# Attention branch projection by seven products of quarters, with the sums of both factors made during the mLSTM

## The chip, the cores and the metric

The kernel runs on one core of one Trainium2 chip. The metric is the device time of one execution in microseconds. Before the change three runs took 1968.49, 1973.42 and 1973.98 us (median 1973.42).

## The reference, cut to what matters

One layer of a diffusion backbone on 1024 tokens of width 1024. Two token mixers work side by side on the same normed input, a windowed attention and a bidirectional mLSTM. Each one's output goes through a projection of its own, is gated, and the two are added:

```
ml = mlstm_readout(ht, mo, ml_norm_w)      # per head of 256: hn = ht * rsqrt(mean(ht^2) + eps) * w; hn * sigmoid(mo)
y  = sigmoid(ga) * (att @ w_branch_att) + sigmoid(gm) * (ml @ w_branch_ml)
x  = x + g1 * (y @ w_out)                  # then the ConvFFN on x, with its own residual
```

All matrices are 32-bit floats. `att`, `ml` and `y` are 1024 x 1024, and so are the three weights. The change concerns `att @ w_branch_att`, and the factor `rsqrt(mean(ht^2) + eps)` of the mLSTM's readout.

## The kernel before, in words

The stages follow one another in `layer_kernel`: startup and context, attention, mLSTM, tail (both branch projections, output projection, second norm), ConvFFN. Every matrix product is made with three matmuls: each operand is split in a high part (a copy on ScalarE, line 44) and a low part (a subtraction on VectorE, line 49), and high x high, high x low, low x high are added in PSUM (`mm3`, lines 90 to 92). The ConvFFN already makes its products by a scheme with seven products of quarters (`product`, lines 1397 to 1399).

A planner orders the instructions of each engine when the kernel is built: an instruction that is written earlier has priority, and one for which data and a buffer are there goes ahead of one that still waits. On the chip each engine then runs its own list in that fixed order. `tc.issue_after(x)` keeps the instructions of a block behind `x` on x's engine. A tile of a pool with `bufs=n` waits until the one n before it has been read for the last time. Loads and stores are issued from SyncE's queue (`nc.sync`) or from ScalarE's (`nc.scalar`).

**The mLSTM** goes head by head (four heads). `proj_kv` makes k and v for all tokens, `proj_q` and `trans_k` make q and the turned k, `states` the first chunk states, and `core` the rest of the chunks of both directions: score products S, outputs o and i, state updates dC. `proj_o` projects the output gate into `sg` (two tiles of 4 x 256 a partition; line 769 writes them), and its matmuls fill TensorE between the small ones of the core. `readout` (lines 1002 to 1015) then handles eight blocks of 128 tokens, one by one: a square with a sum on ScalarE (L1012), scale and power -0.5 on GpSimd (L1013, L1014), and the product with factor and gate on VectorE (L1015). The last of these is kept as `E.turned`. `turn` transposes the result on TensorE (L1023), scales it (L1025) and stores it as `mlT_d` (L1026), in DRAM.

**The attention branch projection** is the first part of `stage_tail`. The attention's output lies turned in DRAM (`attT_d`, 1024 features x 1024 tokens). `load_T` loads it in 16 pieces of 128 x 512 and splits them (`aTh`, `aTl`); `load_w` loads a half of the weight (512 columns) in pieces of 128 x 1024 elements and splits those (`wba0`, `wba1`). Then 16 tiles of 128 columns x 512 tokens follow, each a sum over 8 pieces of 128 features with three matmuls each, in one of two PSUM banks. Each tile's gate (`sga_d`, loaded on ScalarE's queue, L1143) goes through a sigmoid (L1176) and is multiplied with the tile (L1177), and the result is stored to `y1_d` (L1179). Behind these the planner is told to put the loads (L1161) and splits of the mLSTM's output (`mT`) for the next stage. From tile 11 on the first half of the next weight is loaded (`wbm0`).

**The mLSTM branch projection** has the same form (`ym`, gate `sgm`, lines 1199 to 1215): it adds the tile read back from `y1_d`, and VectorE also makes the sums of the modulation (`mod_product`, L210 to L215).

The lines that the prediction speaks of besides: L70 loads the mLSTM's projection weights from SyncE's queue, L1076 the tail's weights, L1116 the attention's output, L1196 the gate row `g1b`.

Of the kernel before, what the change touches and what calls it, by code (L numbers as in the profile page):

```python
# [42 lines left out]
def copy_act(nc, out, in_, scale=1.0):  # L43
    nc.scalar.activation(out, in_, AF.Copy, scale=scale)  # L44


def split_from(nc, hi, lo, src, eng="v"):
    copy_act(nc, hi, src)
    (nc.vector if eng == "v" else nc.gpsimd).tensor_tensor(lo, src, hi.bitcast(F32), op=ALU.subtract)  # L49

# [629 lines left out]
def stage_mlstm(E, st):  # L680
# [4 lines left out]
    psd = E.psx_s.enter_context(tc.tile_pool(name="ps_d", bufs=2, space=PSUM, reuse_waits="tile"))  # L685
    mp = st.enter_context(tc.tile_pool(name="ml1", bufs=1, reuse_waits="tile"))
# [315 lines left out]
    def readout(h):  # L1002
        hf, sgs = H[h]["hf"], H[h]["sg"]
        for t in halves(h):
            if h < MLH - 1:
                nc.scalar.activation(sgs[t], sgs[t], AF.Sigmoid)
            for c in range(4):
                cc = 4 * t + c
                x = hf[:, cc]
                rr = rp.tile([P, 2], F32, tag="rr", name=f"rr{h}_{cc}", bufs=8)  # L1010
                junk = rp.tile([P, 512], F32, tag="mo", name=f"rj{h}_{cc}", bufs=2)
                nc.scalar.activation(junk[:, :DV], x, AF.Square, accum_out=rr[:, 0:1])  # L1012
                nc.gpsimd.tensor_scalar(rr[:, 0:1], rr[:, 0:1], 1.0 / DV, EPS, op0=ALU.mult, op1=ALU.add)  # L1013
                nc.gpsimd.tensor_tensor(rr[:, 1:2], rr[:, 0:1], expo[:, 0:1], op=ALU.pow)  # L1014
                E.turned = nc.vector.scalar_tensor_tensor(x, x, rr[:, 1:2], sgs[t][:, c], op0=ALU.mult, op1=ALU.mult)  # L1015
# [11 lines left out]

    gate_math()
# [6 lines left out]
    proj_q(0)  # L1035
    decays(0)
    for h in range(MLH):
# [9 lines left out]
        if h + 1 < MLH:  # L1047
            proj_q(h + 1)
            trans_k(h + 1)


def stage_tail(E, st):
# [26 lines left out]
    def load_w(src, nm, gate=None, ks=range(2), raws=None):  # L1079
        out = []  # L1080
        for k4 in ks:
            raw = (raws or load_raw(src, nm, [k4]))[k4]
            for k2 in range(2):
# [4 lines left out]
                split_from(nc, h, lo, raw[:, 2 * k2 : 2 * k2 + 2].rearrange("p k c -> p (k c)"))  # L1088
# [16 lines left out]
    def load_T(src, nm, pools, ts=(0, 1), r=None, ks=range(KT)):  # L1105
        r = r or [[], []]
        for t in ts:
            for k in ks:
                if nm == "aT" and t == 0 and k >= 4:

                    if k % 2 == 0:
                        two = op4(f"{nm}r{k}_{t}", F32)
                    raw = two[:, k % 2 * 512 : k % 2 * 512 + 512]
                else:
                    raw = op2(f"{nm}r{k}_{t}", F32)
                E.last = nc.sync.dma_start(raw, src[k * P : (k + 1) * P, t * 512 : (t + 1) * 512])  # L1116
                hl = [x512(f"{nm}{x}{k}_{t}", pool=pools[t][k // 4]) for x in "hl"]
                split_from(nc, hl[0], hl[1], raw)
                r[t].append(hl)
        return r  # L1120

# [8 lines left out]
    def place(i):  # L1130
        n, t, c = tiles[i]
        r0 = n * 512 + c * P
        return slice(r0, r0 + P), slice(t * 512, (t + 1) * 512)

    def ahead(pool, src, tag, nm, bufs):
        got, todo = {}, list(range(16))

        def take(i):
            while todo and todo[0] <= i + 3:
                j = todo.pop(0)  # L1140
                got[j] = pool.tile([P, 512], F32, tag=tag, name=f"{nm}{j}", bufs=bufs)
                rs, ts = place(j)
                nc.scalar.dma_start(got[j], src[rs, ts])  # L1143
            return got.get(i)

        return take

    w = load_w(A["w_ba"][0], "wba0", ks=(0,))
    with tc.issue_after(E.turned.ins):
        aT = load_T(attT_d, "aT", ((0, 1), (2, 6)), (0,), ks=range(4))  # L1150
        w += load_w(A["w_ba"][0], "wba0", ks=(1,))
        load_T(attT_d, "aT", ((0, 1), (2, 6)), (0,), aT, range(4, 8))
    gate = ahead(gp, sga_d, "sg", "sga", 6)
    gate(0)
    load_T(attT_d, "aT", ((0, 1), (2, 6)), (1,), aT)
# [13 lines left out]
    for i, (n, t, c) in enumerate(tiles):  # L1169
        if i == 8:  # L1170
            with tc.issue_after(E.last.ins):
                w = load_w(A["w_ba"][1], "wba1")
        sg = gate(i)
        ps = mm_tile(f"ya{i}")
        mm3(nc, ps, w, aT[t], sl(c * P, P), sl(0, 512))
        ac = nc.scalar.activation(sg, sg, AF.Sigmoid)  # L1176
        dv = nc.vector.tensor_tensor(sg, ps, sg, op=ALU.mult)  # L1177
        rs, ts = place(i)
        sto = nc.sync.dma_start(y1_d[rs, ts], sg)  # L1179
        with tc.issue_after(ac.ins), tc.issue_after(dv.ins), tc.issue_after(sto.ins):  # L1180
            ml_split(i - 2 - 2)
            ml_load(i - 2)
        if i == 11:
            with tc.issue_after(sto.ins):
                wm = load_w(A["w_bm"][0], "wbm0")

# [6 lines left out]
    for i in range(16, 18 + 2):  # L1193
        ml_split(i - 2 - 2)
        ml_load(i - 2)
    nc.sync.dma_start(g1b, E.g_d[0].to_broadcast([P, D]))  # L1196
# [598 lines left out]
```

## Time and profile before

| What | Value |
|---|---|
| Runs | 1968.49, 1973.42, 1973.98 us |
| The profiled execution | 1969.57 us |
| Its span (first to last instruction) | 1967.6 us |
| Granted TensorE clock | 0.999 |
| Branch projection of the attention, first matmul to the next stage's first | 1054.93 to 1145.99 us |
| Waits of TensorE with a named releaser from 690 to 1240 us, the three largest | o for num 2.4, dC for C 1.9, dC for kwl 1.6 us |

The profile is one execution, taken by the hardware profiler. A row of the time line has the start, the duration, the engine (PE is TensorE, PEld its weight loads, DVE VectorE, ACT ScalarE, POOL GpSimd, SPq and ACTq the queues that issue transfers), the line of the kernel, the operation, `out<-in`, shapes and count; in square brackets stands how long the engine had been idle before it, and which instruction released it. Neighbouring rows of one engine overlap, since an instruction starts while the one before it drains: what one costs in a row of equal ones is the distance between starts. Rows of groups have the busy time in all, the mean in ns, and the idle time before. Rows of transfers end with the median time from issue to landing.

### The profile page before, as it was taken

To read this page: it belongs to the slowest core of one execution; us is meant where nothing else is said; L and a number is where in the kernel's file an instruction comes from. 1 tells how busy PE (TensorE), PEld (TensorE's weight loads), DVE (VectorE), ACT (ScalarE), POOL (GpSimd) and SP (SyncE) were. 2 spreads that over 40 slices of the span, in tenths; PEclk is the share of its full clock that TensorE was granted. 3 is DMA by queue.
4 is the path that set the end of the run, shared out by engine and by line. 5 is a ranking of instruction groups with operands and counts; after the bars stand their busy time and mean duration, and the time that the engine had idled before them with its cause. 6 is when DMAs were issued, how large, how long until landed. Compare 5 with 4: busy or idle time off the path is not lost.

```text
span 1967.6 us, 28480 instructions
## 1 busy us (share of the span) xinstructions
PE 1927.2 (98%) x10108; PEld 1649.0 (84%) x10108; DVE 1360.1 (69%) x2734; ACT 965.5 (49%) x1891; POOL 337.2 (17%) x578
## 2 busy tenths in 40 slices
PE   8999999999999999999999999999999999999999
PEld 3988888888888889998997888887888888888887
DVE  2767878868777574646465356559988988996564
ACT  4845556556556354444445332246544454465441
POOL 1223424333332232232221000010000000000000
PEclk9999999999999999999999999999999999999999
DMA  8731222222222211212108664732355444489651
GB/s 307 235 122 55 79 69 73 80 62 79 62 62 81 64 57 39 78 33 79 33 30 272 193 232 149 268 118 75 121 190 203 177 166 174 168 298 336 228 175 64
DMA packets 124013, 264.94 MB, mean 135 GB/s; under 512 B 13904, under 2 KB 38112, under 8 KB 121056
## 3 DMA queue, kind: packets, MB, share of 16 engines
q1 hardware_dynamic: 115232, 247.41, 36.9%
q10 hardware_dynamic: 8640, 15.73, 2.4%
q8 instruction: 79, 1.29, 0.3%
q14 instruction: 62, 0.51, 0.1%
HBM read 197.48 MB, written 65.61 MB: 134 GB/s over the span
## 4 chain that ended last, share of the span: by engine, by line
PE 80%; DVE 7%; DMA 7%; ACT 4%; issue 2%; POOL 1%; SPq 0%; ACTq 0%; POOLq 0%; DVEq 0%
PE pa L1397 4%; PE pa L1399 4%; PE pa L1398 4%; PE pt L623 3%; PE g L92 3%; PE g L91 2%; PE g L90 2%; DMA wmb<-in_w_modB 2%; PE dx L1397 2%; PE dx L1398 2%; PE dx L1399 2%; PE pb L1399 2%; PE pb L1398 2%; PE pb L1397 2%; PE po L617 2%; PE kv L90 2%
## 5 line engine op out<-in xcount | busy, mean ns | idle before, releaser
L604 POOL TENSOR_SCALAR P<-P,st 128x640 f32<-128x640 f32 (+1 forms) x128 | 115.2, 918 | 260.2 <-DVE st L602 177.7
L595 ACT ACTIVATE P<-P,st 128x640 f32<-128x640 f32 (+1 forms) x128 | 102.5, 801 | 24.7 <-DVE st L591 23.7
L591 DVE CUSTOM_DVE_ANT_0 P<-s,maskA,nsink 128x640 f32<-128x640 f32 (+1 forms) x112 | 103.1, 920 | 9.4 <-PE s L588 7.9
L49 DVE TENSOR_TENSOR pl<-pt,ph 128x512 fp32r<-128x512 f32 x152 | 100.8, 686 | 10.2 <-ACT ph L44 9.1
L44 ACT ACTIVATE ph<-pt 128x512 fp32r<-128x512 f32 x152 | 87.5, 597 | 37.1 <-PE pt L623 33.1
L90 PE MATMUL g<-hH,fh 128*128 128x512 f32 x256 | 102.7, 401 | 0.6 <-ACT fh L44 0.6
L92 PE MATMUL g<-hH,fl 128*128 128x512 f32 x256 | 100.6, 393 | 0.4 <-DVE fl L49 0.4
L91 PE MATMUL g<-hL,fh 128*128 128x512 f32 x256 | 100.5, 393 | 0.0
L623 PE MATMUL pt<-ident,P 128*128 128x128 f32 x608 | 92.3, 273 | 3.5 <-POOL P L604 3.1
L90 PE MATMUL pq<-w1h,hH 128*128 128x384 f32 (+1 forms) x256 | 87.1, 340 | 0.2 <-DVE t L543 0.2
L90 PE MATMUL kv<-w1h,hH 128*128 128x384 f32 x256 | 86.2, 338 | 1.1 <-ACT w1h L44 1.1
L92 PE MATMUL pq<-w1h,hL 128*128 128x384 f32 (+1 forms) x256 | 86.7, 339 | 0.0
L91 PE MATMUL kv<-w1l,hH 128*128 128x384 f32 x256 | 86.5, 338 | 0.0
L91 PE MATMUL pq<-w1l,hH 128*128 128x384 f32 (+1 forms) x256 | 86.5, 338 | 0.0
L92 PE MATMUL kv<-w1h,hL 128*128 128x384 f32 x256 | 86.2, 337 | 0.0
L623 PEld LDWEIGHTS pt<-ident,P 128*128 128x128 f32 x608 | 71.1, 140 | 11.5 <-POOL P L604 6.5
L90 PE MATMUL mo<-w1h,hH 128*128 128x256 f32 x256 | 72.7, 284 | 0.4 <-ACT sg L769 0.2
L92 PE MATMUL mo<-w1h,hL 128*128 128x256 f32 x256 | 72.2, 282 | 0.0
L91 PE MATMUL mo<-w1l,hH 128*128 128x256 f32 x256 | 72.1, 282 | 0.0
L49 DVE TENSOR_TENSOR dfl<-drf,dfh 128x512 fp32r<-128x512 f32 x55 | 38.0, 691 | 47.4 <-ACT dfh L44 47.4
L1535 ACT ACTIVATE cv<-ua,vecT 128x1024 f32<-128x1024 f32 x22 | 27.4, 1244 | 85.1 <-DVE ua L1508 85.1
L1397 PE MATMUL dx<-dwh,dfh 128*128 128x512 f32 x176 | 68.5, 389 | 0.0
(559 smaller groups left out, 6309.3 us busy)
## 6 DMA issues: line engine op xcount, KB each, us to landing
ur<-in_w_up SPq DMA_DIRECT2D x22, 1024.0 KB, 5.0
wmb<-in_w_modB SPq DMA_DIRECT2D x64, 256.0 KB, 2.9
f_d<-cv SPq DMA_DIRECT2D x22, 512.0 KB, 2.6
wm<-in_w_modA SPq DMA_DIRECT2D x16, 512.0 KB, 8.4
fr<-in_w_g SPq DMA_DIRECT2D x32, 256.0 KB, 3.1
drf<-fs_d SPq DMA_DIRECT2D x15, 512.0 KB, 5.6
drw<-wt_d SPq DMA_DIRECT2D x14, 512.0 KB, 6.3
w1b<-in_w_cx SPq DMA_DIRECT2D x16, 388.0 KB, 4.3
```

What stands on the lines that cost most here:

```text
L44: nc.scalar.activation(out, in_, AF.Copy, scale=scale)
L49: (nc.vector if eng == "v" else nc.gpsimd).tensor_tensor(lo, src, hi.bitcast(F32), op=ALU.subtract)
L90: nc.tensor.matmul(ps, lh[:, ls], rh[:, rs], start=start and i == 0, stop=False)
L91: nc.tensor.matmul(ps, lh[:, ls], rl[:, rs], start=False, stop=False)
L92: nc.tensor.matmul(ps, ll[:, ls], rh[:, rs], start=False, stop=stop and i == n - 1)
L591: nc.vector.tensor_tensor_reduce(pm[:, :W], ps[:, off : off + W], mask[:, :W], scale=ss[:, h : h + 1], scalar=nsink[:, hh : hh + 1], op0=A ...
L595: nc.scalar.activation(pm[:, :W], pm[:, :W], AF.Exp, bias=st4[:, h : h + 1], scale=-1.0, accum_out=st4[:, 4 + h : 5 + h])
L604: nc.gpsimd.tensor_scalar(Ps[h][:, :W], Ps[h][:, :W], st4[:, 12 + h : 13 + h], 1.0, op0=ALU.mult, op1=ALU.mult)
L623: nc.tensor.transpose(pt[:, h * P : (h + 1) * P], Ps[h][:, kb * P : (kb + 1) * P], ident)
L1397: nc.tensor.matmul(ps, lh, rh, start=start and i == 0, stop=False, skip_group_check=True)
L1398: nc.tensor.matmul(ps, lh, rl, start=False, stop=False, skip_group_check=True)
L1399: nc.tensor.matmul(ps, ll, rh, start=False, stop=stop and i == n - 1, skip_group_check=True)
```

## The change

1. *Seven products.* Both factors of `att @ w_branch_att` are cut in quarters of 512 x 512 (features by tokens, features by columns). Four sums of the quarters of each factor are formed, and seven products of 512 x 512 x 512 replace the eight: with b the turned attention output and w the weight, the pairs in `BR` below. A product needs 4 PSUM banks; banks are taken from four pools in two sets (`bankx`, `banky`), which products share in turns, so that two of the additions of the scheme are done in PSUM. The others are done by VectorE into eight tiles, `u2` and `u4`.
2. *Sums in the mLSTM.* `branch_sums` is called eight times: three times before the first head's `decays`, three after the first head, two after the second. A call loads four pieces of 128 x 512 (ScalarE's queue) into the two `sg` tiles of the output gate, makes four sums on VectorE and stores them (SyncE's queue) in `S_ba` or `T_at` in DRAM.
3. *Loads of the stage.* 14 steps, each with two transfers of 512 KB (factor and weight, two k each), each split in two parts per operand; two steps ahead of the matmuls. The operands' tiles, raw and split, come from the same pools as before.
4. *Order around it.* One half of the results stays in `u2` and `u4` for the next stage and isn't stored and read again. Ten of the loads of `mT` come with steps 4 to 13, the rest in the first tiles of the next stage, where `g1b` now follows the weight. That stage uses three PSUM banks in turns in place of two. Gates are prefetched into 8 tiles in place of 6.
5. *Norm factors.* The readout squares four blocks first, makes their four factors with two GpSimd instructions on 128 x 4, and then multiplies the four.

The diff, cut to its core:

```diff
@@ stage_mlstm, readout
+            rr = rp.tile([P, 8], F32, tag="rr", name=f"rr{h}_{t}", bufs=2)
             for c in range(4):
-                cc = 4 * t + c
-                x = hf[:, cc]
-                rr = rp.tile([P, 2], F32, tag="rr", name=f"rr{h}_{cc}", bufs=8)
...
-                nc.gpsimd.tensor_scalar(rr[:, 0:1], rr[:, 0:1], 1.0 / DV, EPS, op0=ALU.mult, op1=ALU.add)
-                nc.gpsimd.tensor_tensor(rr[:, 1:2], rr[:, 0:1], expo[:, 0:1], op=ALU.pow)
-                E.turned = nc.vector.scalar_tensor_tensor(x, x, rr[:, 1:2], sgs[t][:, c], op0=ALU.mult, op1=ALU.mult)
+                nc.scalar.activation(junk[:, :DV], hf[:, 4 * t + c], AF.Square, accum_out=rr[:, c : c + 1])
+            nc.gpsimd.tensor_scalar(rr[:, 0:4], rr[:, 0:4], 1.0 / DV, EPS, op0=ALU.mult, op1=ALU.add)
+            nc.gpsimd.tensor_tensor(rr[:, 4:8], rr[:, 0:4], expo[:, 0:4], op=ALU.pow)
+            for c in range(4):
+                x = hf[:, 4 * t + c]
+                E.turned = nc.vector.scalar_tensor_tensor(x, x, rr[:, 4 + c : 5 + c], sgs[t][:, c], op0=ALU.mult, op1=ALU.mult)
@@ stage_mlstm, new
+    def branch_sums():
+        which, i = SUMS.pop(0)
+        two = [rp.tile([P, 4, DV], F32, tag="sg", name=f"bs{which}_{i}_{j}", bufs=2) for j in range(2)]
+        x, y, z, w = [t.rearrange("p c d -> p (c d)")[:, o : o + 512] for t in two for o in (0, 512)]
+        tt = nc.vector.tensor_tensor
+        if which == 0:
+            wb = A["w_ba"]
+            for o, src in ((x, wb[0, :, i]), (y, wb[1, :, i]), (z, wb[1, :, i + 4]), (w, wb[0, :, i + 4])):
+                nc.scalar.dma_start(o, src)
+            tt(z, y, z, op=ALU.add)
+            tt(y, x, y, op=ALU.subtract)
+            tt(x, z, x, op=ALU.subtract)
+            tt(w, w, x, op=ALU.subtract)
+            dst, res = E.S_ba, (z, x, y, w)
+        else:
+            for o, r, t in ((x, i, 0), (y, i, 1), (w, i + 4, 0), (z, i + 4, 1)):
+                nc.scalar.dma_start(o, E.attT_d[r * P : (r + 1) * P, t * 512 : (t + 1) * 512])
...
+        for j, o in enumerate(res):
+            nc.sync.dma_start(dst[:, j, i], o)
@@
     proj_q(0)
+    for _ in range(3):
+        branch_sums()
     decays(0)
...
             trans_k(h + 1)
+            for _ in range((3, 2, 0)[h]):
+                branch_sums()
@@ stage_tail
+    BR = [
+        (rows(0, t0), cols8(0, 0)),
+        (sums4(E.T_at, 1), sums4(E.S_ba, 1)),
+        (rows(4, t0), cols8(0, 4)),
+        (sums4(E.T_at, 0), sums4(E.S_ba, 0)),
+        (sums4(E.T_at, 2), sums4(E.S_ba, 2)),
+        (rows(4, t1), sums4(E.S_ba, 3)),
+        (sums4(E.T_at, 3), cols8(1, 4)),
+    ]
...
+    early = [branch_operand(i, "w") for i in range(2)]
+    with tc.issue_after(E.turned.ins):
+        ready = [list(zip(branch_operand(i, "a"), early[i])) for i in range(2)]
...
+    for p in range(7):
+        first = p not in (2, 5, 6)
+        ps = banks[p] = (bankx, banky)[p % 2](p) if first else banks[p - 2]
+        for i in (2 * p, 2 * p + 1):
+            if i + 2 < 14:
+                ready.append(branch_operands(i + 2))
+            if i == 11:
                 wm = load_w(A["w_bm"][0], "wbm0")
+            if i >= 4:
+                ml_split(nq - 2)
+                ml_load(nq)
+                nq += 1
+            for j, (a, w) in enumerate(ready[i]):
+                k = i % 2 * 2 + j
+                for c in range(4):
+                    cs = sl(c * P, P)
+                    product(nc, ps[c], [(w[0][:, cs], w[1][:, cs])], [a], first and k == 0, k == 3)
+        for c in range(4):
+            if p == 0:
+                copy_act(nc, u2[c], ps[c])
+            elif p == 1:
+                tt(u2[c], ps[c], u2[c], op=ALU.add)
+            elif p == 2:
+                gated((0, 0), c, ps[c], None)
+            elif p == 3:
+                tt(u4[c], ps[c], u2[c], op=ALU.add)
+            elif p == 4:
+                tt(u4[c], ps[c], u4[c], op=ALU.add)
+                gated((1, 1), c, u4[c], u4[c])
+            elif p == 5:
+                tt(u4[c], ps[c], u2[c], op=ALU.add)
+                gated((0, 1), c, u4[c], u4[c])
+            else:
+                tt(u2[c], ps[c], u2[c], op=ALU.add)
+                gated((1, 0), c, u2[c], u2[c])
...
+        sg, y1 = gate(n, t, c), first(n, t, c) if n == t else (u4, u2)[n][c]
...
+        ps = (mm_tile, mm_tile, E.fl_tile)[i % 3](f"ym{i}")
```

`gated` applies the sigmoid and multiplies, and stores the quarters (0, 0) and (1, 1) to `y1_d`; for the other two its sigmoids are kept behind ScalarE's last split of `wbm0`.

124 lines of the change are left out of this document (64 added, 60 removed).

## The prediction

> **What bounds the kernel now.** I read the page's totals first, then the stages by windows, then TensorE's own order around the edited stage, and last the prices of single instructions.
>
> ```profile
> span 1967.6 us, 28480 instructions
> PE 1927.2 (98%) x10108; PEld 1649.0 (84%) x10108; DVE 1360.1 (69%) x2734; ACT 965.5 (49%) x1891; POOL 337.2 (17%) x578
> PE 80%; DVE 7%; DMA 7%; ACT 4%; issue 2%; POOL 1%; SPq 0%; ACTq 0%; POOLq 0%; DVEq 0%
> ```
>
> TensorE is busy for 98% of the span and holds 80% of the chain that ended last. So a matmul taken out is worth its pitch, and anything else counts only where it makes TensorE wait. The windows show where that can happen (columns: from:to, length, then busy time of PE, PEld, DVE, ACT, POOL, granted clock, DMA share, GB/s):
>
> ```profile
> 684.00:697.00 13.00, 13.00 (x76) 12.99 (x75) 3.19 (x5) 3.35 (x8) 0.00 (x0) 1.00 0.10 34
> 697.00:705.00 8.00, 7.50 (x43) 6.10 (x41) 6.97 (x11) 7.01 (x21) 6.61 (x6) 1.00 0.47 122
> 712.00:747.00 35.00, 32.26 (x243) 29.63 (x243) 32.59 (x107) 19.93 (x52) 18.08 (x41) 1.00 0.11 32
> 765.00:793.00 28.00, 28.00 (x162) 28.00 (x162) 4.80 (x10) 5.56 (x16) 0.00 (x0) 1.00 0.10 29
> 1040.00:1055.00 15.00, 14.10 (x120) 13.68 (x118) 8.84 (x21) 11.23 (x30) 9.72 (x16) 1.00 0.78 258
> 1055.00:1070.00 15.00, 13.34 (x54) 9.04 (x53) 10.04 (x16) 10.92 (x20) 0.00 (x0) 1.00 0.93 305
> 1070.00:1090.00 20.00, 20.00 (x90) 16.57 (x89) 6.92 (x11) 5.38 (x8) 0.00 (x0) 1.00 0.91 308
> 1055.00:1146.00 91.00, 89.06 (x387) 71.42 (x386) 34.69 (x49) 32.95 (x54) 0.00 (x0) 1.00 0.72 238
> ```
>
> Three things are to be seen. The branch projection (1055 to 1146) uses VectorE for 34.69 of 91 us, but the DMA engines are at 0.91 to 0.93 for its first 35 us. A head's core (712 to 747) is VectorE's: 32.59 of 35. Between the cores the projections of k and v (765 to 793) leave VectorE, ScalarE, GpSimd and the DMA engines nearly empty while TensorE is full.
>
> **The change, part by part.** *The products.* Sixteen tiles of 8 x 3 matmuls are 384; seven products of 4 banks x 4 x 3 are 336, all 128x512 as before. From TensorE's order:
>
> ```profile
> 1051.92 1.61 PE L1023 MATMUL mt<-ident,hf 128*128 128x128 f32 x11
> 1054.41 0.76 PE L1023 MATMUL mt<-ident,hf 128*128 128x128 f32 x5 [0.88 <-DVE hf L1015]
> 1054.93 0.71 PE L90 MATMUL ya<-aTh,wba0h 128*128 128x512 f32 x2
> 1064.73 0.50 PE L90 MATMUL ya<-aTh,wba0h 128*128 128x512 f32 x1 [1.01 <-ACT aTh L44]
> 1095.77 0.39 PE L90 MATMUL ya<-aTh,wba0h 128*128 128x512 f32 x1
> 1101.67 0.39 PE L92 MATMUL ya<-aTh,wba0l 128*128 128x512 f32 x1
> 1145.99 0.39 PE L90 MATMUL ym<-mTh,wbm0h 128*128 128x512 f32 x1
> ```
>
> The rows at 1095.77 and 1101.67 are 26 matmuls apart, so one costs 0.227 us. The 48 removed ones are worth 10.9 us, and 336 take 76.3 us. The stage lasted 1145.99 - 1054.93 = 91.06 us, 384 x 0.227 = 87.2 of it matmuls and 3.9 waits, most in the first 10 us: operands came in by one k while each k fed only three matmuls. After the change each k feeds four banks (12 matmuls, 2.7 us), so that wait should shrink.
>
> *The readout.* The factor chain of one block was 0.49 + 0.55 us on GpSimd, eight times for the last head; now it is once per four blocks.
>
> ```profile
> 1045.64 0.19 ACT L1012 ACTIVATION_READ_ACCUMULATOR rj<-hf 128x1 f32 x1
> 1051.01 1.21 DVE L49 TENSOR_TENSOR wba0l<-wba0r,wba0h 128x1024 fp32r<-128x1024 f32 x1
> 1051.22 1.41 POOL L1014 TENSOR_TENSOR rr<-rr,expo 128x1 f32<-128x1 f32 x1
> 1052.13 0.39 ACT L769 ACTIVATE sg<-mo 128x256 f32<-128x256 f32 x1 [0.97 <-PE mo L92]
> 1052.71 0.49 POOL L1013 TENSOR_SCALAR rr<-rr 128x1 f32<-128x1 f32 x1
> 1053.28 0.55 POOL L1014 TENSOR_TENSOR rr<-rr,expo 128x1 f32<-128x1 f32 x1
> 1053.87 0.48 DVE L1015 SCALAR_TENSOR_TENSOR hf<-hf,rr,sg 128x256 f32<-128x256 f32 x1 [0.72 <-POOL rr L1014]
> ```
>
> The last square ended at 1045.83, the last factor at 1053.83. Without that queue the last product waits only for the last gate at 1052.52, so it ends near 1053.1, inside the 1.61 us of the first eleven transposes. The 0.88 us wait before the last five goes: -0.9. What is late next is the last output-gate matmul at 1051.9, which is TensorE's own. In the other heads these steps have TensorE work beside them: nothing.
>
> *VectorE in the branch stage.*
>
> ```profile
> 1058.91 1.90 DVE L49 TENSOR_TENSOR aTl<-aTr,aTh 128x512 fp32r<-128x512 f32 x3 [1.09 <-ACT aTh L44]
> 1147.15 3.50 DVE L49 TENSOR_TENSOR wbm0l<-wbm0r,wbm0h 128x1024 fp32r<-128x1024 f32 x3 [5.10 <-ACT wbm0h L44]
> L1177 DVE TENSOR_TENSOR sga<-ya,sga 128x512 f32<-128x512 f32 x15 | 10.3, 689 | 28.2 <-PE ya L92 28.2
> ```
>
> Back to back a 128x512 costs 0.63 and a 128x1024 1.17. In the stage come 52 splits of operands (32.8), 36 combinations and gatings (22.7), 8 splits of the mLSTM output (5.0) and 4 of the next weight (4.7): 65 us under 76.3 of TensorE. That fits on average. The fifth product asks 5.0 + 5.0 + 1.3 = 11.3 and the sixth 5.0 + 4.7 + 1.3 + 5.0 = 16.0 in 10.9 us each, the seventh only 6.3, so VectorE goes into the mLSTM-branch projection about a microsecond late. Behind its sixth combination, which overwrites tiles that a store must have read first, wait those weight splits. I take 0 for it (bounds 0 and 2), since the store has a whole product of 10.9 us and landed in 4.0 (row below).
>
> *Transfers in the branch stage.*
>
> ```profile
> aTr<-attT_d SPq DMA_DIRECT2D x16, 256.0 KB, 5.3
> sga<-sga_d ACTq DMA_DIRECT2D x16, 256.0 KB, 3.5
> y_d<-sga SPq DMA_DIRECT2D x16, 256.0 KB, 4.0
> wbm0r<-in_w_bm SPq DMA_DIRECT2D x4, 512.0 KB, 7.2
> ```
>
> Before, the stage moved 91 us x 238 GB/s = 21.7 MB. After, the operands of pieces 2 to 13 are 24 transfers of 512 KB (12.6 MB), the gates 4.2, the stored half of the result 2.1, the mLSTM output's stores and ten loads 3.7, the next weight 2.1, modulation weights and gate row 1.3, and reads ahead for the next stage about 2: 28 MB. Between 1040 and 1055 the engines stood at 0.78 of their time, and the gate row (0.5 MB) now moves behind the weight, so 2 to 4 MB of it can come early. 24 to 26 MB at 308 GB/s (0.91 busy) take 78 to 84 us, against 76.3 of matmuls. So this is the disputed term: from nothing, if the transfers for the next stage step aside, to 12 us, if the weight's 7.2 us landing adds itself to the 84. I take 4.7 us of waits, a stage of 81, nearest to the middle of the row of 308 GB/s. [...]
>
> *The sums in the mLSTM.* Eight calls, each 4 loads on ScalarE's queue, 4 VectorE steps of 0.63, 4 stores on SyncE's: 20 us of VectorE, 64 transfers, 16.8 MB. Five of the eight come after a readout, where TensorE has 28 us of projections with VectorE at 4.80; three come before the first core.
>
> ```profile
> 761.63 1.67 DVE L1015 SCALAR_TENSOR_TENSOR hf<-hf,rr,sg 128x256 f32<-128x256 f32 x4 [0.99 <-issue]
> 773.84 0.42 DVE L49 TENSOR_TENSOR VL<-kv,VH 128x256 fp32r<-128x256 f32 x1 [3.77 <-ACT VH L44]
> 792.94 0.37 SPq L70 DMA_DIRECT2D w1r<-in_w_mlqo  x1
> ACT mo L1025 <- DMA mlT_d<-mo: 6.0, 3, 2.3
> ```
>
> The gate tiles that the sums borrow are free at 763.3. One call is a load (3.5), its steps (2.5) and a store (4.0), 10 us; three are 30, until 794, before the next core. The stores pass SyncE's last q/o weight load (792.94), which needs its slot only then. A wait of up to 3.77 us on VectorE or ScalarE is covered there, since the k/v eviction is that early. The first group falls at 684 to 714: VectorE has 10 us free to 697, then 6.97 of 8 are taken, so its last steps can meet the first core. I take +1 for the eight calls (bounds 0, as the free time holds all of it, and +6, two calls' VectorE time of 5 in a core plus one late gate tile).
>
> GpSimd has a word in that: the factor at 1051.22 took 1.41 us instead of 0.55 with a two-input VectorE step of 1.21 us beside it. [...] All 32 sum steps are of that kind. [...]
>
> *Sum.* -10.0 for the stage (91.06 to 81), -0.9, +1, 0 for the next stage's start: -9.9. The profiled execution took 1969.57 us (span 1967.6 and 1.97 around it): 1959.7. It lies 3.85 under the median, 1973.42, of runs from 1968.49 to 1973.98; half of that put on gives **1961.5**.
>
> **The rivals.** *Paced by transfers* (chance 0.26): the stage takes 84 us and the weight for the next lands late, 85 to 91 in all; gain 0 to 6, time 1964 to 1971 on the same footing. For it: 0.93 busy already now, and every product needs 2.1 MB per 10.9 us (193 GB/s) beside 15 MB of other traffic. Against: ten raw tiles, five pieces' worth, let loads run ahead.
>
> *Nearly no waits* (0.12): the stage takes 77 to 78; 1969.57 - 13.5 - 0.9 + 0.5 = 1955.7, near 1957 with the half. For it: four matmul banks per operand, and three result banks in the next stage in place of two. Against: the 28 MB.
>
> *Slower: the sums hold up ScalarE's queue* (0.10). Calls of one group share two tiles, so five times (2 + 2 + 1) a load on ScalarE's queue waits for the stores of the call before, up to 10 us after its own predecessor, and evictions of PSUM lie behind it. The row of 6.0 us in 3 waits shows ScalarE held up this way by a store. It decides from where such a wait is longer than 3.77 us or falls in a core. At 4 us in the open five times it costs 20: 1959.7 - 1 + 20 = 1978.7, near 1980.5. Against: the tiles come free 50 us ahead of the next core.
>
> **How the numbers follow.** The forecast's own case, stage 78 to 84, has 0.52 and gives 1957 to 1967. A measurement here tells about 0.3% from no change: 5.9 us, so faster means under 1967.5, slower over 1979.3. Faster: 0.52 + 0.12 + 0.10 of the transfers' 0.26 = 0.74. The same: 0.16 of it and 0.01 of the slower case, 0.17. Slower: 0.09. The range 1956 to 1970 leaves out the slow case, and a tip of two others.
>
> **What would show it.** Right: 336 matmuls on the seven products' lines, the first of them near 1054 plus what the mLSTM gained or lost, the first mLSTM-branch matmul 81 us later, DMA share near 0.9 throughout, waits of TensorE there for operands' splits released by DMA, no wait for the last hf; sums near 684 to 712, 764 to 794 and 862 to 890. Wrong: a core of head 0 longer than now, ScalarE waiting on stores of the sums, or TensorE waiting for VectorE in the fifth and sixth product.

## The result, and the profile after

The changed kernel took 1955.34 us (median of six runs, 1951.16 to 1959.55) beside 1970.49 us for the kernel before (six runs on the same chip, 1965.64 to 1973.98): a ratio of 0.9923, 95% interval 0.9908 to 0.9938. It is faster, by 15.1 us. The forecast was 1961.5 us, in a range of 1956 to 1970, and the terms of its sum came to 9.9 us gained. The profiled execution took 1951.16 us, the shortest of the six, 18.4 less than the profiled one of before. The terms below are therefore compared as lengths of stages in two profiles, and the whole as medians.

The totals of the page after:

```profile
span 1949.3 us, 28563 instructions
PE 1912.9 (98%) x10060; PEld 1641.0 (84%) x10060; DVE 1405.1 (72%) x2818; ACT 980.0 (50%) x1927; POOL 315.7 (16%) x530
```

TensorE has exactly 48 matmuls fewer (10108 to 10060) and is 14.3 us less busy, of which the 48 are 10.9. It still holds 98% of the span, now a shorter one. VectorE has 45.0 us more work, most of it beside TensorE's.

The windows of the changed kernel, for the places that the prediction looked at (from:to, length, busy time of PE, PEld, DVE, ACT, POOL, granted clock, DMA share, GB/s):

```profile
684.00:697.00 13.00, 10.87 (x65) 10.52 (x64) 5.18 (x8) 3.32 (x9) 0.00 (x0) 1.00 0.68 223
712.00:747.00 35.00, 32.29 (x242) 29.64 (x241) 32.70 (x112) 20.47 (x55) 18.29 (x42) 1.00 0.12 31
765.00:793.00 28.00, 28.00 (x162) 28.00 (x161) 12.91 (x22) 5.56 (x16) 0.00 (x0) 1.00 0.65 225
1055.00:1070.00 15.00, 15.00 (x68) 12.41 (x67) 12.79 (x21) 13.67 (x27) 0.00 (x0) 1.00 0.99 346
1070.00:1090.00 20.00, 20.00 (x90) 16.58 (x89) 15.32 (x25) 13.96 (x26) 0.00 (x0) 1.00 1.04 395
1052.60:1129.60 77.00, 76.99 (x344) 63.59 (x343) 61.79 (x96) 51.43 (x90) 0.00 (x0) 1.00 0.99 356
1129.60:1217.40 87.80, 87.80 (x393) 72.83 (x392) 59.71 (x88) 29.25 (x45) 0.00 (x0) 1.00 0.39 132
```

The branch stage is the sixth row, and the seventh is the next stage but for its last microsecond. It lasts 77.0 us, 336 x 0.227 = 76.3 of it matmuls, and TensorE is busy for 76.99 of the 77.00. The transfers move 77.0 us x 356 GB/s = 27.4 MB at a share of 0.99: a little more than the 24 to 26 MB that were counted, at a higher rate than was assumed. The stage's first 15 us, where TensorE was busy for 13.34 before, are full. The second group of sums (765 to 793) took VectorE from 4.80 to 12.91 us and left TensorE at 28.00 of 28. The first group did not: from 684 to 697 TensorE lost 2.13 of 13 us. A core of a head (712 to 747) has VectorE at 32.70 as before (32.59).

Where TensorE turns from the mLSTM to the branch stage, in its own order after the change:

```profile
1051.38 1.49 PE L1025 MATMUL mt<-ident,hf 128*128 128x128 f32 x12
1052.62 0.48 PE L1487 MATMUL ya<-bah,bwh 128*128 128x512 f32 x1
1053.11 0.66 PE L1025 MATMUL mt<-ident,hf 128*128 128x128 f32 x4
1053.52 0.48 PE L1488 MATMUL ya<-bal,bwh 128*128 128x512 f32 x1
```

The last four transposes of the mLSTM's output stand behind the first product's first matmul now, and no wait stands before any of the rows. From the last output-gate matmul to the stage's first matmul it was 3.12 us, and is 1.37.

The stage lengths side by side, from the first and last starts of each tile's matmuls in the two profiles (us; a positive difference is time gained):

| Stretch | Before | After | Gained |
|---|---|---|---|
| First kv matmul of the group to first q matmul | 41.6 | 44.1 | -2.5 |
| First q to last output-gate matmul | 353.2 | 353.4 | -0.2 |
| Last output gate to the branch stage | 3.12 | 1.37 | 1.75 |
| Branch stage (ya to ym) | 91.1 | 77.0 | 14.1 |
| Next stage (ym to op) | 90.1 | 88.8 | 1.3 |
| Output projection (op to pa) | 93.9 | 93.3 | 0.6 |

These add up to 15.1. Ahead of the first row the changed kernel's profile was 3.2 us earlier at the same point (653.8 for 657.0), where no step of the change runs yet, so that part of the 18.4 us isn't the change's.

### The profile page after: what moved, and what is told of

It is laid out like the page before. It is cut to its first block, busy times and chain, and to the rows that moved or that the text cites. A ratio compares the mean times of both kernels' runs of the same rounds, so it can differ in the third digit from the quotient of the medians.

```text
span 1949.3 us, 28563 instructions
## 1 busy us (share of the span) xinstructions
PE 1912.9 (98%) x10060; PEld 1641.0 (84%) x10060; DVE 1405.1 (72%) x2818; ACT 980.0 (50%) x1927; POOL 315.7 (16%) x530
## 4 chain that ended last, share of the span: by engine, by line
PE 87%; DVE 5%; DMA 3%; ACT 3%; issue 1%; POOL 1%; SPq 0%; POOLq 0%; ACTq 0%; DVEq 0%
PE pa L1487 4%; PE pa L1488 4%; PE pa L1489 4%; PE pt L624 3%; PE g L93 3%; PE g L92 3%; PE g L91 3%; PE dx L1489 2%; PE dx L1488 2%; PE dx L1487 2%; PE pb L1487 2%; PE pb L1488 2%; PE pb L1489 2%; PE po L618 2%; PE pq L91 2%; PE pq L92 2%
## 5 line engine op out<-in xcount | busy, mean ns | idle before, releaser
L1625 ACT ACTIVATE cv<-ua,vecT 128x1024 f32<-128x1024 f32 x22 | 27.4, 1244 | 85.5 <-DVE ua L1598 85.5
```

## The experiments

Ratios are to the kernel before on the same chip. Kernels of one group below ran on one chip.

### First group: each part alone

**The factors in fours alone** (the kernel before, with the readout of the changed one):

```diff
...
-                nc.gpsimd.tensor_tensor(rr[:, 1:2], rr[:, 0:1], expo[:, 0:1], op=ALU.pow)
...
+            nc.gpsimd.tensor_tensor(rr[:, 4:8], rr[:, 0:4], expo[:, 0:4], op=ALU.pow)
...
```

> The kernel before with one part of the change alone: the norm factors of four blocks at a time in the readout. Theory A (the change gained the 48 matmuls and, around them, waits that its new order takes away): the last factor comes some 8 us earlier, TensorE's wait of 0.88 us for the last hf goes and the first branch matmul comes 0.9 to 1.8 us earlier; but the branch stage still fetches its operands one k at a time, so of this 0.5 to 1.5 us are left at the end: 1969 +- 2 against 1970.5. Rival (the readout alone opened the way for the early operands, and so holds most of the 4 us beyond the matmuls): first branch matmul 2 us earlier and the stage 3 us shorter, 1966.

Measured: 1972.06 us, ratio 1.0005 (0.999 to 1.0021). The part is worth nothing that shows, where both theories expected a gain. From the last output-gate matmul to the stage it was 2.7 us (3.1 before), and the stage itself was 94.3 us for 91.1, so what little was gained ahead of it is not kept.

**The sums alone** (the kernel before with the eight calls of `branch_sums`, whose results nobody reads):

```diff
+    for _ in range(3):
+        branch_sums()
     decays(0)
...
+            for _ in range((3, 2, 0)[h]):
+                branch_sums()
```

> The kernel before with the eight calls of sums added in the mLSTM, their results not used by anything. Theory A: 20 us of VectorE and 16.8 MB lie in stretches that are TensorE's; the one visible loss is a wait of k/v matmuls near 690 behind a VectorE step that waits for its load (2.1 us in the changed kernel's profile); +0 to +2.5 us. Rival (the sums hold up ScalarE's queue, the slower case of the prediction): +6 or more, with waits of ScalarE on stores in the cores.

Measured: 1974.86 us, ratio 1.0024 (1.001 to 1.0038). The ratio makes that 4.7 us more, between the two theories. The stretch from the first kv to the first q matmul alone is 46.4 us for 41.6. Its windows at the first group, and the wait behind them:

```profile
690.00:695.00 5.00, 3.83 (x22) 3.51 (x21) 0.00 (x0) 0.77 (x3) 0.00 (x0) 1.00 0.70 231
695.00:700.00 5.00, 3.15 (x10) 3.16 (x11) 3.34 (x6) 0.83 (x1) 0.00 (x0) 0.69 0.52 200
```

```profile
DVE bs L1040 <- DMA bs<-in_w_ba: 11.8, 3, 8.4
```

VectorE, which had been counted as having room, did nothing at all for five microseconds: the sum at the head of its list waited 8.4 us for its load. TensorE lost 3.0 of the 10 us, and the granted clock of the second window, in which it came back, was 0.69.

**Eight products in the new form** (the changed kernel with plain quarters, two products per result, and no sums):

```diff
...
+    QS = [(0, 0), (1, 1), (0, 1), (1, 0)]
+    BR = [(rows(k, (t0, t1)[t]), cols8(n, k)) for n, t in QS for k in (0, 4)]
...
```

> The changed kernel with eight plain products of quarters in place of seven, in the same form (four banks per operand, 512 KB transfers), and no sums in the mLSTM. Theory A: the branch stage takes 384 x 0.227 = 87.2 and under 1.5 us of waits, 88 to 88.7 against 91.1 before and 77.0 with seven, so the form alone is worth about 2.5 us of the stage and the products 10.9; the whole lies 9 to 11 us above the changed kernel (the sums' 2 us wait is saved). Rival B (the transfers set the pace): 16.8 MB of operands in 32 transfers run at what the engines give, the stage is 91 or more, and the form is worth nothing.

Measured: 1965.3 us, ratio 0.9975 (0.9963 to 0.9988). Its stage and the one that follows it:

```profile
1053.50:1141.30 87.80, 87.78 (x391) 72.56 (x390) 55.45 (x86) 54.49 (x96) 0.00 (x0) 1.00 0.95 344
1141.30:1235.80 94.50, 90.77 (x402) 74.87 (x400) 60.28 (x86) 28.60 (x44) 0.00 (x0) 0.98 0.36 117
```

384 matmuls are 87.2 us, so 0.6 of waits is left where the kernel before had 3.9: the form alone takes 3.3 us of waits away, without a matmul fewer. The seven products then take 10.8 (87.8 to 77.0). This kernel loses 5.7 us again in the next stage: a matmul waits 3.7 us for a product that VectorE gates late, and the matmuls behind that wait run at a lower granted clock (0.66 from 1145 to 1150). The changed kernel has no such wait. That the whole lies 10.0 us above the changed kernel, as expected, is therefore in part luck, since nobody expected this loss.

**Shorter runs of memory for the sums** (2 KB for each partition and piece in place of 4):

```diff
-            nc.sync.dma_start(dst[:, j, i], o)
+            nc.sync.dma_start(dst[:, i, j], o)
```

> The changed kernel with the sums laid out in DRAM so that a load of two k takes runs of 2 KB in place of 4 KB; the same transfers, the same bytes. Rival B, in its sharper form (the prediction's rate of 308 GB/s belonged to transfers in runs of 2 KB, and only runs of 4 KB lifted it to the 356 GB/s that kept the transfers off the path): the rate in the stage falls to 310 to 325 GB/s, the stage grows by 4 to 7 us, waits of TensorE on operands appear. Theory A (the rate in the kernel before was set by how its loads were issued, not by the runs): rate 345 or more, stage 77 to 78, the whole within 1 us of the changed kernel.

Measured: 1958.09 us, ratio 0.9932 (0.9913 to 0.9951), and a stage of 76.9 us at 350 GB/s, without a wait for operands. The rate doesn't hang on the longer runs. The median is 2.7 us over the changed kernel's, where at most 1 was expected, but the intervals overlap and the stage shows nothing of it. Transfers of 256 KB in place of 512 were not tried.

### Second group: how near the edge the transfers stand, where the sums stand, and the readout again

**More bytes in the stage** (with each of the 12 steps that load operands one more load, of 512 or of 256 KB, that nobody needs, behind the weight's):

```diff
+        with tc.issue_after(E.last.ins):
+            nc.sync.dma_start((g1b, g2b)[i % 2].rearrange("p (k c) -> p k c", k=2), A["w_o"][0][:, i % 4 * 2 : i % 4 * 2 + 2])
```

> The changed kernel with one more load of 512 KB in each of the steps 2 to 13 of the branch stage, behind the step's weight load on SyncE's queue, into the gate rows' tiles, which nothing reads until they are loaded anew (6.3 MB more). Theory A, as the runs so far leave it: transfers of the branch stage are not on the path, but they stand close to it (27.4 MB in 77.0 us at a share of 0.99, best stretches near 400 GB/s, so room for about 31 MB): 33.7 MB at 390 to 400 GB/s take 84 to 86 us, the stage grows by 7 to 9 us and TensorE waits for operands. Rival (a share of 0.99 says only that some packet is always queued, there is room left): the stage stays within 1.5 us of 77.

> The same with 256 KB a step (3.1 MB more, 30.5 MB in all). Theory A: just within what the engines give, 390 to 400 GB/s for 76 to 78 us; the stage grows by 0 to 2 us. Rival with room: nothing. If the stage grows by 4 or more, the engines' rate of 356 was already the limit, and the change stood at its edge.

Measured, with 512 KB: 1963.9 us, ratio 0.9963 (0.9949 to 0.9977); with 256 KB: 1965.65 us, 0.9964 (0.9947 to 0.9981). The stage with 512 KB, the two windows in its middle, the window of its longest wait, and the wait:

```profile
1057.50:1142.40 84.90, 80.62 (x343) 65.31 (x342) 58.30 (x90) 48.10 (x83) 0.00 (x0) 0.96 0.98 359
1080.00:1100.00 20.00, 20.00 (x90) 16.55 (x89) 13.68 (x22) 11.95 (x21) 0.00 (x0) 1.00 0.99 362
1100.00:1120.00 20.00, 20.00 (x90) 16.55 (x89) 11.72 (x19) 7.74 (x14) 0.00 (x0) 1.00 1.01 370
1130.00:1140.00 10.00, 6.95 (x19) 5.15 (x18) 8.54 (x12) 5.95 (x9) 0.00 (x0) 0.67 0.99 382
```

```profile
PE ya L1489 <- ACT bwh L44: 3.8, 2, 3.1
```

At 362 to 370 GB/s TensorE still has all it needs (20.00 of 20). With 6.3 MB more in all, though, the stage takes 7.9 us longer. TensorE stands still for 4.3 of them (84.90 less 80.62), most of it before a split whose piece landed late, at 1133.25. The other 3.6 (80.62 for 76.99) are matmuls that take longer, behind the longest wait, at a granted clock of 0.67. The expected 84 to 86 us came, but not by the expected 390 to 400 GB/s: the stage moved 359.

With 3.1 MB more the stage is only 1.1 longer (78.1). The next one is 94.8 for 88.8, with one wait of 3.7 us for the split of its second weight half. That isn't a late transfer: the four pieces were issued by 1142.0 and landed within 7.9 us, and from 1180 to 1190 the DMA engines stood at 0.28 to 0.36. The split stood in ScalarE's list behind a sigmoid that waited for its gate:

```profile
1185.28 0.63 ACT L1297 ACTIVATE sgm<-sgm 128x512 f32<-128x512 f32 x1 [3.60 <-DMA sgm<-sgm_d]
1185.82 1.04 ACT L44 ACTIVATE wbm1h<-wbm1r 128x1024 fp32r<-128x1024 f32 x1
```

Why the gates ran later in this kernel than in the changed one was not settled. So the rival of the transfers was no fancy: in the stage it costs 1.1 us with 3.1 MB more and 7.9 with 6.3, and the changed kernel has little room.

**The sums later** (no call before the first core, then three, three and two):

```diff
-    for _ in range(3):
-        branch_sums()
...
-            for _ in range((3, 2, 0)[h]):
+            for _ in range((3, 3, 2)[h]):
```

> The changed kernel with no call of the sums ahead of the first core, three after each of the heads 0 and 1 and two after head 2. Theory A: the first group's third call costs a wait of 2.1 us of TensorE near 690 (5 us in the kernel with the sums alone), the calls between the cores cost nothing, and head 2 has the same 28 us free: 2 to 3 us shorter than the changed kernel, ratio to before 0.991 or less, no wait of k/v matmuls near 690. Rival (the sums cost nothing on the whole, the wait near 690 is paid back by the q projection's own wait later): the same as the changed kernel, 0.9923.

Measured: 1955.27 us, ratio 0.992 (0.9907 to 0.9932). The wait near 690 is gone (42.1 us from the first kv to the first q matmul), and the whole is the same: no gain that shows. From the first q to the last output-gate matmul this profile has 355.9 us for 353.4.

**The factors block by block in the changed kernel**:

```diff
...
-            nc.gpsimd.tensor_tensor(rr[:, 4:8], rr[:, 0:4], expo[:, 0:4], op=ALU.pow)
...
+                nc.gpsimd.tensor_tensor(rr[:, 1:2], rr[:, 0:1], expo[:, 0:1], op=ALU.pow)
...
```

> The changed kernel with the readout as before, block by block. Theory A: the chain on GpSimd ends 8 us later, TensorE waits for the last hf again and the first branch products wait for splits that are queued behind the last product on VectorE; the path from the last output-gate matmul to the first branch matmul grows from 1.3 to 2.5 to 3.5 us, the whole by 1 to 2.5 us. Rival (the readout is worth nothing here either, as it was alone): within 0.5 us.

Measured: 1956.23 us, ratio 0.9928 (0.9911 to 0.9944), and 1.42 us from the last output gate to the stage, for 1.37 with the factors in fours. The expectation of 1 to 2.5 us lost fell. Here too the first product's first matmul stands ahead of the last four transposes (1058.33, and 1058.77), and nothing waits. So the start is earlier because the products' first operands are there, whichever way the factors are made.

### Third group: inside the form

**Two PSUM banks in the next stage:**

```diff
-        ps = (mm_tile, mm_tile, E.fl_tile)[i % 3](f"ym{i}")
+        ps = mm_tile(f"ym{i}")
```

> The changed kernel, with the mLSTM branch projection's tiles in two PSUM banks in turns, as before the change, in place of three. That projection took 90.1 us to the next stage's first matmul before the change and 88.8 after it; 384 matmuls at 0.227 us are 87.2. Theory A, the third bank takes the waits away: back to 90 us, so 1 to 1.5 us more in that stretch, and TensorE waits there for VectorE's read of a bank. Rival B, the 1.3 us came from the next weight's load, which is issued 28 us earlier now, or from the tiles that stay in SBUF: 88.8 +- 0.3 with two banks too. The whole is no help here, 1 us is under what it can tell: 1955.3 +- 3 by both.

Measured: 1957.31 us, ratio 0.9923 (0.9902 to 0.9944), the next stage 88.8 us: the third bank is not where the 1.3 us came from. The kernel before with the factors in fours alone had 88.8 in this stage too, and the other runs of the changed form have 88.8 to 89.8, but for the two with a named wait there (eight products, and 256 KB more). So the 1.3 us is about what this stage varies by, and no part of the change is shown to have made it.

**Bank by bank** (the four pieces of a product inside, the banks outside):

```diff
-            for j, (a, w) in enumerate(ready[i]):
-                k = i % 2 * 2 + j
-                for c in range(4):
...
+        for c in range(4):
...
+            for k, (a, w) in enumerate(ready[2 * p] + ready[2 * p + 1]):
...
```

> The changed kernel with the same 336 matmuls in another order: each product's four banks one after the other, the four steps of 128 features inside, so that the first bank asks for all four pieces of both operands within 12 matmuls (2.7 us) and not within 36 (8.2 us). Theory A, the order by pieces with four banks on each is what removed 3 us of waits at the stage's start: the first bank of the first product waits again for its third and fourth pieces, the gap from the last output-gate matmul or the stage's start grows by 2 to 5 us, and the stage from its first matmul to the next stage's first is 79 to 82 us in place of 77.0; in the later products each operand pair comes ahead by two steps and nothing is added, or up to 1 us each. Whole: 1957 to 1962. Rival B, what removed them is only that fewer bytes a matmul are asked for, or an earlier load: the stage is 77 to 78 us, whole 1955 +- 3.

Measured: 1958.57 us, ratio 0.9933 (0.991 to 0.9957), a stage of 79.4 us. The size is the expected one, the place is not. At the start TensorE is full; the waits come in the sixth and seventh product (from 1113 and from 1124). The windows of this kernel, and its three waits in TensorE's order:

```profile
1058.00:1068.00 10.00, 9.98 (x46) 7.77 (x46) 8.45 (x14) 10.00 (x20) 0.00 (x0) 1.00 0.84 275
1110.00:1120.00 10.00, 9.85 (x43) 7.73 (x42) 9.25 (x14) 5.92 (x10) 0.00 (x0) 1.00 0.97 331
1120.00:1130.00 10.00, 8.88 (x38) 6.72 (x37) 10.00 (x16) 9.20 (x17) 0.00 (x0) 1.00 1.00 358
```

```profile
1116.25 0.50 PE L1488 MATMUL ya<-bah,bwl 128*128 128x512 f32 x1 [0.15 <-DVE bwl L49]
1126.27 0.50 PE L1488 MATMUL ya<-bah,bwl 128*128 128x512 f32 x1 [0.88 <-DVE bwl L49]
1127.47 0.50 PE L1488 MATMUL ya<-bah,bwl 128*128 128x512 f32 x1 [0.24 <-DVE bwl L49]
```

From 1120 to 1130 VectorE is busy for 10.00 of 10 us. That is the crowding that the prediction reckoned for the late products (16.0 us of VectorE's work in the 10.9 of the sixth), and the split of the last pieces lies behind it. Piece by piece a product can begin with one split of four, and the crowding stays hidden (TensorE is busy for 76.99 of 77.00 us); bank by bank its first bank wants all four. The start needs no such order: a product of quarters asks for four pieces in 10.9 us, where the first tile before asked for eight in 24 x 0.227 = 5.4. That last sentence is read from the code and the stage's start; no run changes that alone.

**Two calls of sums before the first core** (then three and three):

```diff
-    for _ in range(3):
+    for _ in range(2):
...
-            for _ in range((3, 2, 0)[h]):
+            for _ in range((3, 3, 0)[h]):
```

> The changed kernel with the eight calls of the sums put two ahead of the first core, three after the first head and three after the second, in place of three, three and two; the same work. Theory A, the third call of the first group is what costs time near 690 us, since its loads wait for the tiles of the call before, VectorE waits 7.6 us for them and the k and v projections' PSUM stays full: no VectorE wait over 4 us there, no wait of TensorE's kv matmuls for VL, the stretch from the first kv matmul of the group to the first q matmul 42 us in place of 44.1, whole 1 to 3 us shorter (ratio to before 0.991 +- 0.001). Rival B, the wait is that of the first call's own loads, whatever follows: the VL wait of about 2 us stays. Rival C, it moves to the second head's group, where three calls now end later: a wait appears near 880 to 900 us.

Measured: 1952.26 us, ratio 0.9901 (0.9882 to 0.9921), 41.0 us from the first kv to the first q matmul, and no wait for `VL` there. No wait of TensorE appears near 880 to 900 in its place.

### Fourth group: what the sums cost, on one chip

**The changed kernel, and the version with two early calls, once more:**

> The changed kernel as it is, beside the next two on one chip, as their measure: 1955 +- 2 us by every theory, with the stretch from the first kv matmul to the first q matmul at 44 to 46 us and a branch stage of 77.0 us.

> The kernel with two calls of the sums before the first core, three after each of the first two heads, now beside the changed kernel on one chip. Theory A, the third early call holds up VectorE and through it the k and v projections: 2 to 4 us shorter than the changed kernel in the whole, 41 us from the first kv matmul to the first q matmul in place of 44 to 46. Rival, the earlier measurement fell low by chance: within 1 us of it in the whole, though the stretch is shorter.

**No sums** (the eight calls left out, plain quarters read in their place):

```diff
...
-            for _ in range((3, 2, 0)[h]):
-                branch_sums()
...
-        (sums4(E.T_at, 1), sums4(E.S_ba, 1)),
+        (rows(0, t1), cols8(1, 0)),
...
```

> The changed kernel without the eight calls that make the sums; the seven products read plain quarters of both factors in place of the sums (so what they add up to is left out). What the sums cost as they stand: theory A, 4 to 6 us in the whole, most of it near 690 and the rest in transfers and VectorE work beside the other heads' steps, so 1950 +- 2 us; branch stage 77.0 us still, since it reads as many bytes. Rival, the sums are hidden but for 1 us, as the prediction had it, and the stretch near 690 is made up later: 1954 to 1956. If so the eight plain products' 88 us stage stands alone for the rest.

| Kernel | Median, us | Ratio (95%) | First kv to first q, us |
|---|---|---|---|
| Changed | 1956.10 | 0.992 (0.9906 to 0.9935) | 46.5 |
| Two early calls | 1953.69 | 0.9908 (0.989 to 0.9925) | 42.1 |
| No sums | 1951.99 | 0.99 (0.9884 to 0.9915) | 42.0 |

The sums cost 4.1 us in the whole by these medians, and these profiles put it in the first stretch (46.5 us for 42.0; 44.1 to 46.5 in all profiles with three early calls). Moving one call gained 2.4 by the medians. That isn't shown clear of the noise: the intervals of the first two rows overlap, and the version without early calls has a first stretch as short (42.1) and the changed kernel's whole. It is the second time that the version with two early calls has the lower ratio (0.9901 the first time, 0.9923 for the changed kernel on another chip). Its two profiles don't show the gain, though: from the first q to the last output-gate matmul they take 358.9 and 356.3 us, where the changed kernel's two take 353.4 and 354.1. TensorE is idle there for 10.1 and 10.5 us, as in the changed kernel (9.9 and 10.7). What differs is the busy time of the same 2301 or 2302 matmuls, 349.0 and 346.1 us for 343.7 and 343.6, with seven and four windows of 5 us at a granted clock of 0.50 to 0.96 in it, for two and one in the changed kernel's. So a profile that meets such windows hides the 3 to 4 us that the first stretch gains, and the medians are too few to settle it.

What the stretch does show is how a sum stops TensorE. VectorE's order in the profiled changed kernel, near 690:

```profile
680.12 0.69 DVE L1047 TENSOR_TENSOR bs<-bs,bs 128x512 f32<-128x512 f32 x1
...
682.93 0.41 DVE L49 TENSOR_TENSOR VL<-kv,VH 128x256 fp32r<-128x256 f32 x1
690.90 0.69 DVE L1044 TENSOR_TENSOR bs<-bs,bs 128x512 f32<-128x512 f32 x1 [7.56 <-DMA bs<-in_w_ba]
691.51 0.42 DVE L49 TENSOR_TENSOR VL<-kv,VH 128x256 fp32r<-128x256 f32 x1
```

and who waits for the row at 691.51, in TensorE's:

```profile
691.98 0.44 PE L91 MATMUL kv<-w1h,hH 128*128 128x384 f32 x1 [2.13 <-DVE VL L49]
```

The second call makes its last sum at 680.12, and the first sum of the third heads VectorE's list at 683.3. It borrows the same two tiles, so its loads had to wait for the stores of the second call: the last store was issued at 680.84 and landed at 684.00, the last two loads were issued at 684.02 and 684.40. The sum waits 7.56 us for them. The split of v that frees a kv bank stands behind it in the list, and TensorE stops when it has no bank left. In the second profile of the version with two early calls this stretch is full:

```profile
685.00:700.00 15.00, 15.00 (x91) 14.86 (x91) 5.77 (x12) 4.96 (x12) 1.99 (x5) 1.00 0.38 118
```

In the second profile of the changed kernel the stop was 2.67 us, and more followed it:

```profile
690.00:695.00 5.00, 2.50 (x8) 2.50 (x9) 3.34 (x6) 0.59 (x3) 0.00 (x0) 0.68 0.45 174
695.00:700.00 5.00, 5.00 (x22) 4.97 (x21) 1.92 (x2) 1.74 (x4) 0.00 (x0) 0.64 0.55 160
```

In the 5 us after the stop TensorE is busy throughout, at a granted clock of 0.64, and the stretch is 46.5 us for the 44.1 of the first profile.

## Why the prediction was off: 1961.5 us forecast, 1955.34 measured

**The term of the transfers in the branch stage is the step that failed.** It was 4.7 us of waits, and measured 0.7. The bytes weren't the reason: of 28 MB asked for, 24 to 26 were to move in the stage, and 27.4 did. The rate was: 308 GB/s at a share of 0.91 came from 20 us of the kernel before in which TensorE waited for nothing, and was read as what the transfers could do. After the change they gave 356 over the whole stage and 395 over 20 us of it. The profile of the kernel before already had faster stretches, one of them in the same stage:

```profile
1130.00:1135.00 5.00, 5.00 (x24) 4.14 (x23) 2.39 (x3) 1.58 (x2) 0.00 (x0) 1.00 1.01 397
1780.00:1800.00 20.00, 20.00 (x90) 16.53 (x90) 10.15 (x16) 10.76 (x20) 0.00 (x0) 1.00 1.04 396
```

Why the same engines moved only 305 GB/s at 0.93 in the first 15 us of that stage, where TensorE did wait, stays open: the attention's output came in transfers of 256 KB there and of 512 after the change, issued at other times, and of these differences only the length of the runs was tested. The rival "nearly no waits" (a stage of 77 to 78, chance 0.12) is what came about.

**The rival of the transfers** was rightly seen and wrongly placed: 3.1 MB more cost 1.1 us in the stage, and 6.3 MB more 7.9, of which 3.6 are slower matmuls behind the waits.

**The products.** 48 matmuls at 0.227 were 10.9 us; the eight-product run against the changed kernel gives 10.8 for the stage. Right.

**The shape of the operand waits.** "That wait should shrink" was right (3.9 to 0.6, by the eight-product run). That each piece feeds four banks was the reason given, and it isn't the one that counts at the start: bank by bank the start is as full. What the order by pieces does hide is VectorE's crowding late in the stage, 1.3 us of named waits in a stage that is 2.4 us longer without it.

**The readout.** The wait of 0.88 us went, as stated, and 1.8 us were gained at that place for 0.9. The cause given was wrong: made block by block the factors leave 1.42 us there for 1.37. It is the first products going ahead of the last transposes.

**The sums in the mLSTM**, +1 with bounds 0 and 6, measured 4.1 and 4.7 in two ways: inside the bounds, at the wrong end. The prediction looked for them in a core and on ScalarE's queue. ScalarE waited once for a load of the sums, 2.9 us; in a profile of the version with two early calls it waited 11.4 in three, and no wait of TensorE names it. The cost came through VectorE, in stretches where it had little to do: a waiting sum holds up what stands behind it, and room in the windows is not room in the list. They began at 655, too, and not at 684.

**VectorE in the stage.** It was busy for 61.79 of the 77 us (65 reckoned), and no wait of TensorE for it shows. It went into the next stage over 4 us late, not about one: its last gating ended at 1134.05. The next stage's start lost 0, as taken, since nothing there waited for it.

**How the errors combined.** On the two profiles the stage gave 4.1 us more than forecast and its start 0.9 more; the sums took 1.7 more (2.5 + 0.2 for 1), and the two stages behind were 1.9 shorter with no step for it: -9.9 - 4.1 - 0.9 + 1.7 - 1.9 = -15.1. The forecast time was 6.2 us over the measured one: 5.2 by these terms, and the rest by its footing, which put the kernel before at some 1971.4 us where the median beside the result was 1970.49. The medians on two chips (15.1 and 16.9 us gained) were not taken apart further. A run without sums gains 21.0 by the medians of the second chip, while its profile is 17.7 shorter than that of before: the profiled execution before, at 1969.57, lies 3.4 under that chip's median of 1972.97.

## What to carry to other kernels

A transfer rate read where nothing waited for the transfers is a floor (308 GB/s here, with 395 over 20 us after the change), so bound it from above as well before pricing waits by it: look for the fastest stretch of the same profile. Then test how many bytes are left to the edge, since the next change spends them. An operation that is moved into an engine's idle time still stands in that engine's list: price its own wait for data (7.56 us here, which stopped TensorE for 2.13), and name what is queued behind it. When products share operands, give the order that lets matmuls begin with the first piece, as it hides bursts of the engine that prepares the pieces (a stage of 77.0 us here, and of 79.4 bank by bank).

## What the runs showed of the hardware that was not expected

The granted clock fell after short stops of TensorE. A stop of 2.67 us near 692 was followed by 0.64 in the next 5 us, in the second profile of the changed kernel; a stop of 2.13 us at the same place in its first profile was not, and stayed at 1.00. The length doesn't decide it. Of the eight profiles of the changed form with this stop, those with 2.02, 2.24, 2.38, 2.65 and 2.67 us have a granted clock of 0.64 to 0.71 in the window from 695 to 700, and those with 2.13, 2.70 and 2.81 us have 1.00 there and behind it. The shortest (with 512 KB more):

```profile
695.00:700.00 5.00, 5.00 (x20) 5.00 (x21) 4.04 (x6) 1.69 (x2) 0.00 (x0) 0.66 0.68 227
```

and the window behind the longest (with two banks):

```profile
700.00:705.00 5.00, 5.00 (x33) 4.42 (x32) 3.94 (x7) 3.09 (x6) 1.84 (x3) 1.00 0.71 210
```

The second profile of the version with two early calls showed it elsewhere, near the ends of cores:

```profile
740.00:745.00 5.00, 3.13 (x15) 3.08 (x15) 3.77 (x14) 2.75 (x10) 4.32 (x8) 0.70 0.00 0
940.00:945.00 5.00, 4.35 (x20) 4.35 (x21) 4.05 (x17) 2.80 (x9) 2.05 (x8) 0.50 0.00 0
```

The kernel before has it there too (0.81 from 935 to 940), so the change didn't bring it. The runs of the changed kernel have a mean clock from 0.995 (1959.55 us) to 0.999 (1951.16 us). By an estimate 0.004 of 1955 us is 7.8 us, about the whole spread of 8, so these dips go with much of it. Why some of these stops were followed by such a window and others of like length were not, no run here shows.
